# The first tile's output stored in pieces of 2, 11 and 12 tokens in place of 13 and 12, in a copy-and-scale kernel

## The chip, the cores and the metric

The kernel runs on one core of a Trainium2 chip. The metric is the device time of one execution in microseconds (us), the median of several runs. Engines that matter here: VectorE (DVE in the profile), ScalarE (ACT), and 16 DMA engines, which move all transfers. A transfer is issued from a queue: SP's (SyncE's, SPq in the profile, q1 in its DMA rows) or ACT's (ACTq, q10). "GB/s" counts bytes moved by all 16 DMA engines; MB are 10^6 bytes and KB in the rows of transfers 1,024 bytes.

## What is computed

```python
batch, seq, hidden, n_experts = 16, 1024, 512, 8
k = 2
# x: [16, 1024, 512] float32, expert_weights: [16, 1024, 2] float32
x_expanded = x[:, :, np.newaxis, :].repeat(k, axis=2)
weights = expert_weights[..., np.newaxis]
return (x_expanded * weights).astype(np.float32)
```

Each of 16,384 tokens is a row of 512 floats. It is written twice, scaled by each of its two weights. 33.55 MB are read and 67.11 MB written; expert_indices isn't used.

## The kernel before

**Tiles.** The tokens are spread over 128 partitions, 128 tokens to a partition. They are cut into five tiles of 25 tokens a partition (`groups`) and a rest of 3 (`LAST`). In what follows "a token" means one token on every partition: 2 KB of input and 4 KB of output on each. Transfers go by rows of one partition: a load of 25 tokens is 128 packets of 51,200 bytes, a store of 13 tokens 128 packets of 53,248.

**Memory.** Two input buffers (`x_pool`) take turns, so the load of tile i + 2 waits until tile i is multiplied. One output ring, `o_ring`, holds exactly 25 tokens of output; every tile writes the same places, so a piece of tile i + 1 can be multiplied only when the stores of tile i that read those places have landed. The rest has a buffer of its own for its input (`z_tile`), and its output goes to the start of the ring. The 128 weights pairs of a partition stand in `w_tile`.

**Loads.** `load` (L66 to L89) issues them on ACT's queue: tile 0 in pieces of 9 and 16 tokens (`FIRST`), tile 1 whole. Behind the first piece, `weights` issues the weights on SP's queue in three transfers: those of tile 0 (L97, 25 KB, 128 rows of 200 bytes), those of tiles 1 to 4 (L99, 100 KB, 512 rows of 200 bytes), those of the rest (L106, 3 KB, 128 rows of 24 bytes). Behind the multiplication of tile 0 ACT issues the load of tile 2 (L79) and that of the rest (L87, 768 KB, 128 rows of 6,144 bytes); a one-column copy (L76) keeps the latter behind tile 0.

**Multiplying and storing.** `emit` (L150 to L154) goes through the pieces of a tile, given as a list of cuts and a list of shares. `fill` has VectorE multiply the first `v` tokens of a piece, in instructions of up to 4 tokens (`CH`, L129), and ACT the others, one instruction for each token and weight (L119). Then SP issues the store of the piece (L154). Tiles 0 and 1 have pieces of 13 and 12 tokens, tiles 2 to 4 of 9, 8 and 8. Of the first 13 tokens VectorE takes 9 and ACT 4, of the next 12 VectorE 9 and ACT 3.

**Order.** Each engine runs its instructions in the order in which they stand; the framework adds the semaphore waits. For the transfers of SP and ACT it has eight completion semaphores, which the transfers take in turn. A transfer whose semaphore was last used by another one is issued only once that one has landed (where the engine doesn't know this already by an earlier wait).

The lines that matter most:

```python
    SHARES = [[9, 9], [9, 8], [9, 8, 8]]
...
    for i in range(2):
        load(i)
    for i, (done, n) in enumerate(tiles):
        cuts = [0, 13, n] if i < 2 else [0, 9, 17, n]
        emit(loaded[i], rows(of, done, n), done * k, cuts, SHARES[min(i, 2)])
        load(i + 2)
```

Of the kernel before, what the change touches and what calls it, by code (L numbers as in the profile page):

```python
# [1 line left out]

# [4 lines left out]


@with_exitstack
def kernel(  # L10
    ctx: ExitStack,
    tc: tile.TileContext,
    x: bass.AP,
    expert_indices: bass.AP,
    expert_weights: bass.AP,
    out: bass.AP,
):
    nc = tc.nc

    batch, seq, hidden = x.shape  # L20
    k = expert_weights.shape[-1]
    P = nc.NUM_PARTITIONS
    ntok = batch * seq
    assert ntok % P == 0
    A_TOTAL = ntok // P

    f32 = mybir.dt.float32
    row = k * hidden
    CH = 4


    groups = [25, 25, 25, 25, 25]
    TX = max(groups)
    LAST = 3
    FIRST = [9, 16]
    SHARES = [[9, 9], [9, 8], [9, 8, 8]]
    assert sum(groups) + LAST == A_TOTAL

    xf = x.rearrange("b s h -> (b s) h")
    of = out.rearrange("b s k h -> (b s) (k h)")  # L40
    wf = expert_weights.rearrange("b s k -> (b s) k")

    w_pool = ctx.enter_context(tc.tile_pool(name="w_pool", bufs=1))
    x_pool = ctx.enter_context(tc.tile_pool(name="x_pool", bufs=2))
    o_pool = ctx.enter_context(tc.tile_pool(name="o_pool", bufs=1))

    w_tile = w_pool.tile([P, A_TOTAL * k], f32)
    o_ring = o_pool.tile([P, TX * row], f32)

    def rows(of_all, done, T):  # L50
        return of_all[done * P : (done + T) * P, :].rearrange(
            "(p a) n -> p (a n)", a=T
        )


    if LAST:
        z_pool = ctx.enter_context(tc.tile_pool(name="z_pool", bufs=1))
        z_tile = z_pool.tile([P, LAST * hidden], f32)

    tiles = []  # L60
    done = 0
    for n in groups:
        tiles.append((done, n))
        done += n

    loaded = []  # L66

    def load(i):
        if i >= len(tiles):
            return  # L70
        done, n = tiles[i]
        x_tile = x_pool.tile([P, TX * hidden], f32)
        src = rows(xf, done, n)
        steps = FIRST if i == 0 else [n]
        if i == 2 and LAST:
            nc.scalar.copy(out=z_tile[:, :1], in_=o_ring[:, TX * row - 1 :])  # L76
        for e, step in enumerate(steps):
            at = sum(steps[:e])
            nc.scalar.dma_start(  # L79
                out=x_tile[:, at * hidden : (at + step) * hidden],  # L80
                in_=src[:, at * hidden : (at + step) * hidden],
            )
            if i == 0 and e == 0:
                for g in range(3):
                    weights(g)
        if i == 2 and LAST:
            nc.scalar.dma_start(out=z_tile, in_=rows(xf, A_TOTAL - LAST, LAST))  # L87
        loaded.append(x_tile)


    T0 = groups[0]
    G = len([n for n in groups[1:] if n == T0])
    head = (1 + G) * T0

    def weights(e):
        if e == 0:
            nc.sync.dma_start(out=w_tile[:, : T0 * k], in_=rows(wf, 0, T0))  # L97
        elif e == 1:
            nc.sync.dma_start(  # L99
                out=w_tile[:, T0 * k : head * k].rearrange("p (g n) -> p g n", g=G),  # L100
                in_=wf[T0 * P : head * P, :].rearrange(
                    "(g p a) n -> p g (a n)", g=G, p=P
                ),
            )
        else:
            nc.sync.dma_start(  # L106
                out=w_tile[:, head * k :], in_=rows(wf, head, A_TOTAL - head)
            )

    def product(engine, o_tile, t, x_in, c, m):  # L110

        o = t * row
        if engine is not None:
            for e in range(m * k):
                out_e = o_tile[:, o + e * hidden : o + (e + 1) * hidden]
                in_e = x_in[:, e // k * hidden : (e // k + 1) * hidden]
                w_e = w_tile[:, c + e : c + e + 1]
                if engine is nc.scalar or engine is nc.any and (c + e) % 3 == 2:
                    nc.scalar.mul(out=out_e, in_=in_e, mul=w_e)  # L119
                else:  # L120
                    nc.vector.tensor_scalar(
                        out=out_e,
                        in0=in_e,
                        scalar1=w_e,
                        scalar2=None,
                        op0=mybir.AluOpType.mult,
                    )
            return
        nc.vector.tensor_tensor(  # L129
            out=o_tile[:, o : o + m * row].rearrange(  # L130
                "p (t k h) -> p t k h", t=m, k=k
            ),
            in0=x_in[:, : m * hidden]
            .rearrange("p (t h) -> p t h", t=m)
            .unsqueeze(2)
            .to_broadcast([P, m, k, hidden]),
            in1=w_tile[:, c : c + m * k]
            .rearrange("p (t k) -> p t k", t=m)
            .unsqueeze(3)
            .to_broadcast([P, m, k, hidden]),  # L140
            op=mybir.AluOpType.mult,
        )

    def fill(o_tile, x_in, c, m, v):
        for t in range(0, v, CH):
            u = min(t + CH, v)
            product(None, o_tile, t, x_in[:, t * hidden : u * hidden], c + t * k, u - t)
        product(nc.scalar, o_tile, v, x_in[:, v * hidden :], c + v * k, m - v)

    def emit(src, dst, c, cuts, shares):  # L150
        for at, to, v in zip(cuts, cuts[1:], shares):
            o_tile = o_ring[:, at * row : to * row]
            fill(o_tile, src[:, at * hidden : to * hidden], c + at * k, to - at, v)
            nc.sync.dma_start(out=dst[:, at * row : to * row], in_=o_tile)  # L154

    for i in range(2):
        load(i)
    for i, (done, n) in enumerate(tiles):
        cuts = [0, 13, n] if i < 2 else [0, 9, 17, n]
        emit(loaded[i], rows(of, done, n), done * k, cuts, SHARES[min(i, 2)])  # L160
        load(i + 2)
    emit(
        z_tile,
        rows(of, A_TOTAL - LAST, LAST),
        (A_TOTAL - LAST) * k,
        [0, LAST],
        [LAST],
    )

# [1 line left out]
_INS = ['x', 'expert_indices', 'expert_weights']  # L171
_OUTS = [((16, 1024, 2, 512), 'float32')]


# [23 lines left out]
```

## Time and profile before

| | us |
|---|---|
| median of 3 runs | 239.63 |
| lowest and highest | 239.58 and 239.79 |
| the profiled execution | 239.66 |
| its span in the profile | 237.9 |
| VectorE busy | 123.8 |
| ACT busy | 20.2 |

The span runs from the first to the last instruction of the program. The page of the profile gives busy times by engine, rows of 40 equal slices of the span, the traffic of the DMA queues, the chain of work that ended last, groups of instructions by line with busy time, mean time and the idle time before them, and the transfers with the median time from issue to landing. A view of the traffic can be had for any window; in it a packet counts whole in the place where it starts, so a window of a few us that large packets straddle shows a rate that is too high or too low, and only windows of small packets or long windows can be read as rates. Lines such as L129 are those of the kernel listed above.

### The profile page before, as it was taken

How to read it: one execution, taken by the hardware profiler on the slowest of the kernel's cores; microseconds unless marked ns; L12 is line 12 of the kernel's file. 1: busy time of each engine (PE TensorE's matmuls, PEld its weight loads, DVE VectorE, ACT ScalarE, POOL GpSimd, SP SyncE). 2: the span in 40 equal slices, each digit the busy share in tenths (PEclk: the TensorE clock that was granted, in tenths of full speed). 3: DMA queues.
4: the chain of work that ended last, by engine and by line, in shares of the span. 5: the costliest groups of instructions: out<-in, count | busy, mean ns of one | idle time of the engine just before them, and what ended most of it. 6: DMA issues, size and time to landing. Idle time of an engine off the chain costs nothing.

```text
span 237.9 us, 167 instructions
## 1 busy us (share of the span) xinstructions
DVE 123.8 (52%) x33; ACT 20.2 (8%) x32; POOL 0.2 (0%) x4
## 2 busy tenths in 40 slices
DVE  0499800000059293089505999493096999865000
ACT  0008900000052160000000000000000000000000
POOL 0000000000000000000000000000000000000000
DMA  7999999999999999999999999899999999999996
GB/s 259 450 422 467 467 433 415 415 391 450 439 397 397 417 430 438 496 446 407 403 419 426 484 419 474 364 452 452 439 409 430 413 435 436 477 398 441 441 441 265
DMA packets 3840, 100.80 MB, mean 424 GB/s; under 512 B 1152, under 2 KB 1152, under 8 KB 1280
## 3 DMA queue, kind: packets, MB, share of 16 engines
q1 hardware_dynamic: 2832, 67.24, 65.7%
q10 hardware_dynamic: 1008, 33.55, 33.2%
HBM read 33.69 MB, written 67.11 MB: 424 GB/s over the span
## 4 chain that ended last, share of the span: by engine, by line
DMA 68%; DVE 18%; ACT 3%; issue 2%; ACTq 0%; DVEq 0%; SPq 0%
DMA out_dram<-o_ring 60%; DVE o_ring L129 18%; DMA x_tile<-in_x_dram 7%; ACT o_ring L119 2%; ACT L119 1%; ACTq L79 0%; DVEq L129 0%; SPq L154 0%; ACTq L119 0%
## 5 line engine op out<-in xcount | busy, mean ns | idle before, releaser
L129 DVE TENSOR_TENSOR o_ring<-x_tile,w_tile 128x4096 f32<-128x4096 f32 (+1 forms) x32 | 120.4, 3820 | 91.6 <-DMA out_dram<-o_ring 69.8
L119 ACT ACTIVATE o_ring<-x_tile,w_tile 128x512 f32<-128x512 f32 x30 | 18.7, 708 | 48.1 <-DMA out_dram<-o_ring 48.0
L129 DVE TENSOR_TENSOR o_ring<-z_tile,w_tile 128x3072 f32<-128x3072 f32 x1 | 3.4, 3360 | 2.1 <-DMA out_dram<-o_ring 2.1
L119 ACT ACT_TABLE_LOAD x1 | 1.3, 1283 | 19.0 <-DMA x_tile<-in_x_dram 19.0
L76 ACT COPY z_tile<-o_ring 128x1 f32<-128x1 f32 x1 | 0.2, 191 | 0.0
L182 POOL MEMSET const-bfloat16-1.0<- 128x1 bf16 x1 | 0.1, 102 | 0.0
L182 POOL MEMSET const-uint8-127<- 128x1 uint8 x1 | 0.1, 102 | 0.0
L182 POOL MEMSET const-float32-0.0<- 128x1 f32 x1 | 0.1, 99 | 0.2 <-issue 0.2
L182 POOL MEMSET const-float32-1.0<- 128x1 f32 x1 | 0.1, 99 | 0.0
## 6 DMA issues: line engine op xcount, KB each, us to landing
x_tile<-in_x_dram ACTq DMA_DIRECT2D x4, 6400.0 KB, 30.5
out_dram<-o_ring SPq DMA_DIRECT2D x6, 4096.0 KB, 21.5
out_dram<-o_ring SPq DMA_DIRECT2D x3, 4608.0 KB, 26.8
out_dram<-o_ring SPq DMA_DIRECT2D x2, 6656.0 KB, 33.1
out_dram<-o_ring SPq DMA_DIRECT2D x2, 6144.0 KB, 44.8
x_tile<-in_x_dram ACTq DMA_DIRECT2D x1, 4096.0 KB, 17.8
x_tile<-in_x_dram ACTq DMA_DIRECT2D x1, 2304.0 KB, 8.3
out_dram<-o_ring SPq DMA_DIRECT2D x1, 1536.0 KB, 19.5
```

Of the source, the lines that this page charges most:

```text
L76: nc.scalar.copy(out=z_tile[:, :1], in_=o_ring[:, TX * row - 1 :])
L119: nc.scalar.mul(out=out_e, in_=in_e, mul=w_e)
L129: nc.vector.tensor_tensor(out=o_tile[:, o : o + m * row].rearrange("p (t k h) -> p t k h", t=m, k=k), in0=x_in[:, : m * hidden] .rearrange ...
L182: nc = _bacc.Bacc("TRN2", target_bir_lowering=False, num_devices=1)
```

## The change

Tile 0 is stored in three pieces, of 2, 11 and 12 tokens. VectorE multiplies both tokens of the first piece and 7 of the 11 of the second, ACT the other 4 of these; the 12 tokens stay as they were. The cuts move into a list beside the shares. In all, VectorE multiplies 18 tokens of tile 0 and ACT 7, as before.

```diff
     FIRST = [9, 16]
-    SHARES = [[9, 9], [9, 8], [9, 8, 8]]
+    CUTS = [[0, 2, 13, 25], [0, 13, 25], [0, 9, 17, 25]]
+    SHARES = [[2, 7, 9], [9, 8], [9, 8, 8]]
     assert sum(groups) + LAST == A_TOTAL
...
     for i, (done, n) in enumerate(tiles):
-        cuts = [0, 13, n] if i < 2 else [0, 9, 17, n]
-        emit(loaded[i], rows(of, done, n), done * k, cuts, SHARES[min(i, 2)])
+        form = min(i, 2)
+        emit(loaded[i], rows(of, done, n), done * k, CUTS[form], SHARES[form])
         load(i + 2)
```

All lines behind the new one move down by one (L129 becomes L130, L154 becomes L155). In the compiled program:

- VectorE's first three instructions of tile 0 are of 2,048, 4,096 and 3,072 elements a partition in place of 4,096, 4,096 and 1,024; the others are the same. ACT's instructions are the same.
- SP issues 15 stores in place of 14: 8,192 and 45,056 bytes a partition in place of 53,248, the others as before. The first waits for VectorE alone, the second for VectorE and ACT, as the one of 13 tokens did.
- VectorE's first instruction of tile 1 waits for both stores.
- The transfers take other semaphores from there on. The load of the rest (L88), which had that of the first weights (25 KB), has that of the second (100 KB), and its issue waits for them.

The semaphores, numbered 0 to 7, with the transfers that take each in order (t1a is the first store of tile 1, and so on; s2, s11, s12 and s13 are the stores of tile 0 by their tokens; x3 is the load of tile 3):

| | before | after |
|---|---|---|
| 0 | x0 (9), s12, t2c | x0 (9), x2, x4, last store |
| 1 | weights 25 KB, rest's load, t3a | weights 25 KB, s12, t2c |
| 2 | weights 100 KB, t1a, t3b | weights 100 KB, rest's load, t3a |
| 3 | weights 3 KB, x3, t3c | weights 3 KB, t1a, t3b |
| 4 | x0 (16), t1b, t4a | x0 (16), x3, t3c |
| 5 | x1, t2a, t4b | x1, t1b, t4a |
| 6 | s13, t2b, t4c | s2, t2a, t4b |
| 7 | x2, x4, last store | s11, t2b, t4c |

## The prediction

> **What bounds the kernel now.** I read the head of the page first, then the timeline of the first 70 us, the transfers, and last the DMA traffic of chosen windows. The page's span, VectorE's share and the two DMA rows (40 slices of 5.95 us: busy tenths, then GB/s):
>
> ```profile
> span 237.9 us, 167 instructions
> DVE 123.8 (52%) x33; ACT 20.2 (8%) x32; POOL 0.2 (0%) x4
> ...
> DMA  7999999999999999999999999899999999999996
> GB/s 259 450 422 467 467 433 415 415 391 450 439 397 397 417 430 438 496 446 407 403 419 426 484 419 474 364 452 452 439 409 430 413 435 436 477 398 441 441 441 265
> ```
>
> The 16 DMA engines are busy in every slice; VectorE is busy for half the span. So no compute and no issue is the bound: the kernel ends when the bytes are through, and a change of the time must come from bytes, from the rate of some stretch, or from the two ends. The execution took 239.66 us for its span of 237.9; the median of the runs is 239.63, 0.03 lower.
>
> The timeline of the first 70 us (start, duration, engine; ACTq and SPq are the queues that issue transfers):
>
> ```profile
> 0.72 1.43 ACTq L79 DMA_DIRECT2D x_tile<-in_x_dram  x3
> 0.72 0.37 SPq L97 DMA_DIRECT2D w_tile<-in_expert_weights_dram  x1
> 1.15 0.43 SPq L99 DMA_DIRECT2D w_tile<-in_expert_weights_dram  x1
> 1.62 0.50 SPq L106 DMA_DIRECT2D w_tile<-in_expert_weights_dram  x1
> 9.05 19.77 DVE L129 TENSOR_TENSOR o_ring<-x_tile,w_tile 128x4096 f32<-128x4096 f32 x6 [9.05 <-DMA x_tile<-in_x_dram]
> ...
> 20.27 8.68 ACT L119 ACTIVATE o_ring<-x_tile,w_tile 128x512 f32<-128x512 f32 x14
> 25.30 4.02 SPq L154 DMA_DIRECT2D out_dram<-o_ring  x2
> ...
> 29.05 0.34 ACTq L79 DMA_DIRECT2D x_tile<-in_x_dram  x1
> 29.43 0.46 ACTq L87 DMA_DIRECT2D z_tile<-in_x_dram  x1
> 67.82 2.56 ACT L119 ACTIVATE o_ring<-x_tile,w_tile 128x512 f32<-128x512 f32 x4 [38.65 <-DMA out_dram<-o_ring]
> 67.83 4.42 DVE L129 TENSOR_TENSOR o_ring<-x_tile,w_tile 128x4096 f32<-128x4096 f32 x1 [39.01 <-DMA out_dram<-o_ring]
> ```
>
> The first store is issued at 25.30, but that isn't when it moves. The transfers (line, queue, KB, us from issue to landing), and the traffic from 20 to 48 us (q1 is SP's queue, q10 ACT's: packets, MB, time share):
>
> ```profile
> w_tile<-in_expert_weights_dram SPq DMA_DIRECT2D x1, 100.0 KB, 48.6
> w_tile<-in_expert_weights_dram SPq DMA_DIRECT2D x1, 25.0 KB, 5.5
> w_tile<-in_expert_weights_dram SPq DMA_DIRECT2D x1, 3.0 KB, 50.5
> ```
>
> ```profile
> DMA packets 502, 11.93 MB, mean 426 GB/s; under 512 B 270, under 2 KB 270, under 8 KB 270
> ## 3 DMA queue, kind: packets, MB, share of 16 engines
> q10 hardware_dynamic: 248, 11.88, 98.2%
> q1 hardware_dynamic: 254, 0.05, 0.9%
> ```
>
> From 20 to 48 us SP's queue moves 254 packets of 0.05 MB, weights of some 200 B, one for each of the 248 big packets of ACT's queue. The two take turns packet by packet. So the 100 KB of weights (512 rows) land at 1.15 + 48.6 = 49.75 us and the last 3 KB at 1.62 + 50.5 = 52.1, and the stores issued at 25.30 and after wait behind them until about 51. That decides what an earlier store can do.
>
> Then a stretch stands out. The traffic from 48.9 to 50.7 us, and from 100 to 217 us:
>
> ```profile
> DMA packets 144, 0.44 MB, mean 243 GB/s; under 512 B 73, under 2 KB 73, under 8 KB 144
> ## 3 DMA queue, kind: packets, MB, share of 16 engines
> q10 hardware_dynamic: 72, 0.44, 92.9%
> q1 hardware_dynamic: 72, 0.00, 2.2%
> ```
>
> ```profile
> DMA packets 1478, 50.50 MB, mean 432 GB/s; under 512 B 175, under 2 KB 175, under 8 KB 175
> ```
>
> Here rows of z_tile's load (6,144 B, q10) take turns with the last weights (24 B) at 243 GB/s, where the long stretch of loads and stores goes at 432. The engines count as busy, yet a z row takes 0.929 x 16 x 1.8 / 72 = 0.37 us. Against 432 GB/s this stretch loses 1.8 x (1 - 243/432) = **0.79 us**, the one dip I find behind the start.
>
> **The change, part by part.** *The early store* (2 tokens, 1 MB). Its product is one VectorE instruction from 9.05 us. Shapes by line:
>
> ```profile
> L129 DVE TENSOR_TENSOR o_ring<-x_tile,w_tile 128x4096 f32<-128x4096 f32 x26 | 113.8, 4420 | 91.6 <-DMA out_dram<-o_ring 69.8 <-issue 12.8 <-DMA x_tile<-in_x_dram 9.1
> L129 DVE TENSOR_TENSOR o_ring<-x_tile,w_tile 128x1024 f32<-128x1024 f32 x6 | 7.3, 1218 | 0.0
> L129 DVE TENSOR_TENSOR o_ring<-z_tile,w_tile 128x3072 f32<-128x3072 f32 x1 | 3.4, 3360 | 2.1 <-DMA out_dram<-o_ring 2.1
> ```
>
> 2,048 elements are not in the trace: halfway between 1,218 and 3,360 ns is 2,289. The store is then issued near 9.05 + 2.3 = 11.4 us, 14 us earlier, and moves nothing: it stands behind the weights until about 49. Worth 0. If it did get through early, it would only trade places with loads on engines that are already full. VectorE's first 13 tokens cost 2,289 + 4,420 + 3,360 = 10,069 ns in place of 2 x 4,420 + 1,218 = 10,058: 0.01 us, covered by ACT's eight activations, on which the store at 25.30 waits. Without that cover it would be 0.01 us. The 11 tokens are issued at 25.30 as the 13 were, and the second tile's first instructions now wait for both stores, whose bytes together are the old ones: 0.
>
> *One more transfer.* 128 more packets, 8 to an engine, and one more issue (0.35 us on SP's queue, idle between 2.1 and 25.30, nothing behind it). What a packet costs beside its bytes, from rows of 12 KB alone at the end (233.08 to 236.1 us) against large rows (131 to 232 us):
>
> ```profile
> DMA packets 106, 1.29 MB, mean 427 GB/s; under 512 B 1, under 2 KB 1, under 8 KB 1
> ...
> DMA packets 1368, 43.81 MB, mean 434 GB/s; under 512 B 144, under 2 KB 144, under 8 KB 144
> ```
>
> 1.6% of 12,288 B at 27 GB/s an engine (455 ns) is 7 ns; 8 x 7 = **+0.06 us**, on the path because the DMA engines are. Bounds: 0, and 0.13 at twice that for the smaller rows.
>
> The Trainium skill's page "DMA: Bandwidth & Descriptors", section "Anatomy of one DMA", speaks against this piece: it gives each transfer a fixed 2.0 us, mostly the receipt of its last write. By that the sum below would be 239.0 + 2.0 = 241.0. The stretch from 100 to 217 us, with its 432 GB/s across the ends of some ten transfers, shows that here the next transfer's bytes cover it.
>
> *The moved semaphores.* The added transfer shifts the turn in which transfers take the eight completion semaphores. As compiled, z's load takes the one of the 100 KB of weights where it took that of the 25 KB. Its issue at 29.43, which found its semaphore free, must now wait for those weights: until about 49.7 us, or a little less without z beside them. Behind it on ACT stand the second tile's activations, which wait for the first stores until 67.82: 18 us of cover. If that were gone, ACT's stall of 20 us would reach the load of the fourth tile. z's rows are read only here:
>
> ```profile
> 214.16 3.36 DVE L129 TENSOR_TENSOR o_ring<-z_tile,w_tile 128x3072 f32<-128x3072 f32 x1 [2.13 <-DMA out_dram<-o_ring]
> ```
>
> so z itself may be late by 150 us. The other new pairs of transfers on one semaphore are as far apart as the old ones.
>
> What the delay does to the DMA engines is the term that matters. When the third tile's load ends (by 48.9 its large packets have given way to z's rows, as that window shows), ACT's queue is empty. The last weights have the engines to themselves, then come the 8 KB rows of the early store, and z's rows join at about 50.5, among store rows. The dip's pairing of z rows with 24 B rows is gone: **-0.79 us** if all is regained, 0 if none. Against it stands a gap where the last weights run alone with nothing large to fill the engines. The nearest rows for weights that run with little beside them are from 1.7 to 2.46 us, at the start, and, for 24 B rows just ahead of store rows, from 50.7 to 51.4 us:
>
> ```profile
> DMA packets 71, 0.14 MB, mean 187 GB/s; under 512 B 64, under 2 KB 64, under 8 KB 64
> ...
> DMA packets 119, 0.83 MB, mean 1187 GB/s; under 512 B 76, under 2 KB 76, under 8 KB 107
> ```
>
> The first loses 0.76 x (1 - 187/432) = 0.43 us, from a standing start. The second has 76 tiny packets and shows no loss (packets count whole where they start, hence 1,187). So the gap is 0 to 0.43; the second row is nearer, since requests are already under way, and I take +0.1.
>
> Sum: 239.66 - 0.79 + 0.06 + 0.1 = **239.0 us**, the end being reached earlier because every later store and load runs on full engines. Bounds: 239.66 - 0.79 + 0 + 0 = 238.9, and 239.66 - 0.79 + 0.13 + 0.43 = 239.4; the dip's blurred edges may add 0.2 below.
>
> **The rivals.** *Nothing gained.* The dip is not a matter of z and 24 B rows but of passing from loads to the first store: reads for 53 KB store rows begin while z's rows are still coming. For it: the dip ends where the store's rows begin. Against it: in the late part, loads join stores with no dip. Then the loss returns at the new hand-over, and the time is 239.66 + 0.07 = 239.7. The same time comes out if z's issue is not delayed at all.
>
> *Slower: the 24 B rows are the slow thing.* If each holds its engine, whatever else is queued, 0.79 us x 16 engines / 72 rows = 0.18 us a row, then 8 of them in series on each engine, with no z row to fill in, cost 1.4 us each time they are alone: 239.66 - 0.79 + 1.4 + 0.07 = 240.3. It decides if the rate between 48.5 and 50 falls below 243 GB/s. Against it: the 270 packets under 512 B from 20 to 48 us went by at 426 GB/s in all. The Trainium skill's same page, section "Specifications", says that below 512 B a transfer does a read-modify-write, which would suit this rival; the 200 B rows are below 512 B too and show no such loss.
>
> *Slower: each transfer pays a fixed end.* The end of the 2-token store holds the engines before the 11 tokens start. The time from last byte to landing is not hidden then; the last store bounds its size: its rows still start in the window that ends at 236.1, and the span ends at 237.9, so 1.8 us at most. Time 239.66 - 0.79 + 0.07 + 1.8 = 240.7 at most. Against it stands the 432 GB/s of the long stretch.
>
> **How the numbers follow.** Forecast 0.68; nothing gained 0.23; slow 24 B rows 0.06; fixed end 0.03. About 0.2% (0.48 us) is what a measurement of this kernel can tell from no change, so faster begins below 239.15. Of the forecast's own range, 238.7 to 239.4, about three quarters of the chance lies below that, because only a gap near its upper bound lifts it over: 0.50 faster, 0.18 same. With the first rival, same is 0.41; slower is 0.09. The range for 8 in 10 reaches from 238.6 past the first rival to 239.85, which leaves out the two slower cases and the tails.
>
> **What would show it.** Right: the first store issued near 11.4 us but SP's queue still at 0.05 MB from 20 to 48; z's load issued near 49.5 in place of 29.43; traffic between 48.9 and 50.7 above 400 GB/s; the second tile's VectorE work at about 67.2 in place of 67.83, and everything behind it earlier by the same 0.6. Wrong: z's load still issued at 29.4; or a stretch near 49 us as slow as the old one; or a start of the second tile that is early while the end is not, which would mean a new dip later on.

## The result, and the profile after

| | before | changed |
|---|---|---|
| median of 22 runs each, us | 239.68 | 240.27 |
| lowest and highest, us | 239.46 and 240.09 | 239.56 and 240.91 |
| the profiled execution, us | 239.66 | 240.44 |
| its span, us | 237.9 | 238.7 |

The ratio of changed to before is 1.0018, 95% interval 1.0010 to 1.0026 (the two medians alone would give 1.0025): slower, by a little less than the 0.2% that the prediction took as what can be told from no change. In three later comparisons, each on a chip of its own (11 runs of the changed kernel each), the medians were 0.36, 0.06 and 0.07 us over those of the kernel before, with ratios of 1.0009, 1.0005 and 1.0004, whose intervals all reach 1.0000 or below. The 0.6 us of gain that was forecast appeared nowhere. Of the runs further below, three of the six of e6 were in a slower state, and its ratio leaves them out.

The head of the changed kernel's page: the span, VectorE, and the DMA rows of 40 slices.

```profile
span 238.7 us, 169 instructions
...
DVE 123.8 (52%) x33; ACT 20.2 (8%) x32; POOL 0.2 (0%) x4
...
DMA  7999999999999999999999999999999999999995
GB/s 264 464 450 457 439 414 414 414 404 414 427 426 412 488 455 425 431 403 404 412 508 400 408 434 458 431 406 434 433 432 436 439 434 449 402 462 434 428 397 251
```

As before, the DMA engines are busy throughout. The timeline of its first 70 us:

```profile
8.84 19.76 DVE L130 TENSOR_TENSOR o_ring<-x_tile,w_tile 128x2048 f32<-128x2048 f32 x6 [8.84 <-DMA x_tile<-in_x_dram]
11.16 17.93 SPq L155 DMA_DIRECT2D out_dram<-o_ring  x3
...
28.83 0.34 ACTq L80 DMA_DIRECT2D x_tile<-in_x_dram  x1
50.31 0.33 ACTq L88 DMA_DIRECT2D z_tile<-in_x_dram  x1
67.80 2.56 ACT L120 ACTIVATE o_ring<-x_tile,w_tile 128x512 f32<-128x512 f32 x4 [38.85 <-DMA out_dram<-o_ring]
67.84 4.43 DVE L130 TENSOR_TENSOR o_ring<-x_tile,w_tile 128x4096 f32<-128x4096 f32 x1 [39.24 <-DMA z_tile<-in_x_dram]
```

The early store is issued at 11.16, and the rest's load at 50.31 in place of 29.43, as the moved semaphore demands. (The last line's z_tile is the profile's guess from a semaphore that z shares with the weights. The rest landed 19.0 us after its issue, at 69.3, so VectorE didn't wait for it; ACT's line beside it names the stores.) But the second tile starts at 67.84, where it started at 67.83. By then both kernels have moved nearly the same transfers, so up to there nothing was gained and nothing lost. The traffic from 20 to 48 us shows the early store still waiting behind the weights, as in the kernel before:

```profile
q10 hardware_dynamic: 245, 11.72, 99.9%
q1 hardware_dynamic: 244, 0.05, 0.9%
```

**Where the dip went.** From 49.8 to 51.4 us, where z's rows had crawled, the rows of the early store run at 420 GB/s:

```profile
DMA packets 82, 0.67 MB, mean 420 GB/s; under 512 B 0, under 2 KB 0, under 8 KB 0
```

In the window of the prediction, 48.9 to 50.7 us, the traffic is this, where it was 243 GB/s and more than 400 was to be the sign of the gain:

```profile
DMA packets 284, 0.66 MB, mean 365 GB/s; under 512 B 205, under 2 KB 205, under 8 KB 205
```

Large rows that started before 48.9 us still run into this window and aren't counted in it. So the old dip is gone, and a new one stands right ahead of it. In the window from 46.2 to 47.05 us the last rows of the third tile's load start, one on each engine (16 packets on q10). The view gives the time of the packets that start in it as a share of 16 engines' window. First the kernel before, then the changed one:

```profile
q10 hardware_dynamic: 16, 0.82, 224.3%
```

```profile
q10 hardware_dynamic: 16, 0.82, 320.3%
```

2.243 x 0.85 = 1.91 us for one row before, 3.203 x 0.85 = 2.72 us after. The last row of each engine takes 0.82 us longer: the size of the loss that was to be saved (0.79). The loss has only moved from z's rows to the row ahead.

**Where the time grew.** VectorE's later pieces, released by landed stores; the timeline before, then after:

```profile
127.66 22.90 DVE L129 TENSOR_TENSOR o_ring<-x_tile,w_tile 128x4096 f32<-128x4096 f32 x6 [11.69 <-DMA out_dram<-o_ring]
...
173.01 8.76 DVE L129 TENSOR_TENSOR o_ring<-x_tile,w_tile 128x4096 f32<-128x4096 f32 x2 [10.40 <-DMA out_dram<-o_ring]
```

```profile
127.97 22.90 DVE L130 TENSOR_TENSOR o_ring<-x_tile,w_tile 128x4096 f32<-128x4096 f32 x6 [12.13 <-DMA out_dram<-o_ring]
...
173.75 8.76 DVE L130 TENSOR_TENSOR o_ring<-x_tile,w_tile 128x4096 f32<-128x4096 f32 x2 [10.54 <-DMA out_dram<-o_ring]
...
214.90 3.36 DVE L130 TENSOR_TENSOR o_ring<-z_tile,w_tile 128x3072 f32<-128x3072 f32 x1 [2.12 <-DMA out_dram<-o_ring]
```

The lag behind the kernel before is 0.01 us at 67.8, 0.31 at 128, 0.74 at 173 and 0.74 at 214. It comes up in the stretch where the loads of the fourth and fifth tile run beside stores, far from the changed lines.

A landing is told by 16 semaphore increments, one from each DMA engine, and VectorE waits for the last of them. The trace has the time of each. For the last store of the program, in us:

```
profiled run         its time   mean landing   last landing   last - mean
before                 239.66         236.78         237.06          0.29
changed                240.44         236.85         237.81          0.96
changed again (r)      240.45         236.73         237.81          1.08
changed again (f1)     240.19         236.85         237.56          0.71
changed again (g4)     240.11         236.89         237.48          0.59
```

Each time is the last landing plus 2.60 to 2.64 us. The mean landing is the same within 0.16 us. These are single executions: those of r, f1 and g4 took 0.22 to 0.32 us more than the medians of their runs. What grew in them is the distance of the slowest engine from the others: each of the 16 has 8 of a transfer's 128 rows to move by itself, and the kernel ends with the last of them. The end of the trace's traffic shows it without the semaphores: rows that start from 236.3 to 237.5 us, before and after.

```profile
DMA packets 13, 0.00 MB, mean 0 GB/s; under 512 B 13, under 2 KB 13, under 8 KB 13
```

```profile
DMA packets 16, 0.04 MB, mean 31 GB/s; under 512 B 13, under 2 KB 13, under 8 KB 13
```

Before, only completion packets are left by then. After, three rows of 12 KB are still to come, on engines that lag.

### The profile page after: what moved, and what is told of

It is laid out like the page before. It is cut to its first block, busy times and chain, and to the rows that moved or that the text cites. A ratio compares the mean times of both kernels' runs of the same rounds, so it can differ in the third digit from the quotient of the medians.

```text
span 238.7 us, 169 instructions
## 1 busy us (share of the span) xinstructions
DVE 123.8 (52%) x33; ACT 20.2 (8%) x32; POOL 0.2 (0%) x4
## 4 chain that ended last, share of the span: by engine, by line
DMA 66%; DVE 22%; another core or an unknown queue 2%; issue 1%; SPq 0%; DVEq 0%; ACTq 0%
DMA out_dram<-o_ring 38%; DVE o_ring L130 22%; DMA w_tile<-in_expert_weights_dram 21%; DMA z_tile<-in_x_dram 7%; SPq L98 0%; DVEq L130 0%; SPq L155 0%; ACTq L88 0%
## 5 line engine op out<-in xcount | busy, mean ns | idle before, releaser
L130 DVE TENSOR_TENSOR o_ring<-x_tile,w_tile 128x4096 f32<-128x4096 f32 (+3 forms) x32 | 120.4, 3820 | 92.4 <-DMA out_dram<-o_ring 44.3
L130 DVE TENSOR_TENSOR o_ring<-z_tile,w_tile 128x3072 f32<-128x3072 f32 x1 | 3.4, 3357 | 2.1 <-DMA out_dram<-o_ring 2.1
## 6 DMA issues: line engine op xcount, KB each, us to landing
x_tile<-in_x_dram ACTq DMA_DIRECT2D x4, 6400.0 KB, 30.8
```

What stands on the lines that cost most here:

```text
L130: nc.vector.tensor_tensor(out=o_tile[:, o : o + m * row].rearrange("p (t k h) -> p t k h", t=m, k=k), in0=x_in[:, : m * hidden] .rearrange ...
```

## The experiments

Each time is the median of 11 runs (12 for e7 and g1, 4 for e5; for e6 the lowest and highest of 6) beside runs of the kernel before on the same chip. The ratio is that of the measurement and not of the two medians.

| run | tile 0's pieces | rest's load | us | before, us | ratio, 95% interval |
|---|---|---|---|---|---|
| e1_split_rest_early | 2, 11, 12 | early | 239.94 | 239.72 | 1.0008 (0.9999 to 1.0018) |
| e2_whole_rest_late | 13, 12 | late | 239.85 | 239.72 | 1.0004 (0.9995 to 1.0013) |
| e3_whole_order | 13, 12 | early | 239.85 | 239.72 | 1.0008 (1.0000 to 1.0017) |
| e4_split_6_7_12 | 6, 7, 12 | late | 239.94 | 239.72 | 1.0010 (1.0001 to 1.0019) |
| r_changed_again | 2, 11, 12 | late | 240.14 | 239.78 | 1.0009 (1.0000 to 1.0018) |
| e5_one_weight_row_whole | 13, 12 | early | 245.12 | 239.78 | 1.0228 (1.0210 to 1.0246) |
| e6_one_weight_row_split | 2, 11, 12 | early | 240.82 to 245.43 | 239.78 | 1.0103 (1.0052 to 1.0153) |
| e7_pool_weights_split | 2, 11, 12 | early | 240.11 | 239.78 | 1.0015 (1.0005 to 1.0025) |
| f1_changed | 2, 11, 12 | late | 239.87 | 239.81 | 1.0005 (0.9996 to 1.0014) |
| f2_split_rest_early | 2, 11, 12 | early | 240.06 | 239.81 | 1.0013 (1.0004 to 1.0022) |
| f3_whole_rest_late | 13, 12 | late | 239.80 | 239.81 | 1.0002 (0.9992 to 1.0011) |
| f4_whole_order | 13, 12 | early | 239.94 | 239.81 | 1.0003 (0.9994 to 1.0012) |
| g1_pool_weights_whole | 13, 12 | early | 240.42 | 239.82 | 1.0030 (1.0014 to 1.0047) |
| g2_pool_weights_split | 2, 11, 12 | early | 240.01 | 239.82 | 1.0013 (0.9996 to 1.0029) |
| g3_pieces_13_10_2 | 13, 10, 2 | early | 240.06 | 239.82 | 1.0008 (0.9999 to 1.0017) |
| g4_changed | 2, 11, 12 | late | 239.89 | 239.82 | 1.0004 (0.9995 to 1.0012) |

**One part of the change at a time: e1 to e4.** The first theory, A, was that the late load of the rest takes its small rows out of the passage from loads to stores, so that the stall falls unevenly on large rows. The second, B, was that the 2-token piece itself does it.

e1, against the changed kernel (the rest's load shares its semaphore with weights that land early):

```diff
-                for g in range(3):
+                for g in (0, 2, 1):
                     weights(g)
```

> The changed kernel, with the order of the two later weight transfers exchanged, so that the rest's load shares its semaphore with the 3 KB of weights (landed by some 12 us) and is issued near 29 us again. Theory A (the delay of the rest's load takes its small rows out of the passage from loads to stores, the stall there falls unevenly on one large row of each DMA engine, and the slowest engine ends later): about 239.7, the last store's landings as close as in the kernel before (0.5 us from first to last engine). Theory B (the 2-token piece itself does it: one more transfer, 8 KB rows): about 240.3 as the changed kernel.

e2, against the kernel before (one more transfer moves the semaphores as the split does):

```diff
-            nc.sync.dma_start(
-                out=w_tile[:, head * k :], in_=rows(wf, head, A_TOTAL - head)
-            )
+            for lo in (0, P // 2):
+                nc.sync.dma_start(
+                    out=w_tile[lo : lo + P // 2, head * k :],
+                    in_=rows(wf, head, A_TOTAL - head)[lo : lo + P // 2, :],
+                )
```

> The kernel before, tile 0 still in pieces of 13 and 12, with the 3 KB of weights loaded as two transfers of 64 partitions each: the same rows, one more transfer, which moves the rest's load to the semaphore of the 100 KB of weights, so that it is issued near 50 us. Theory A: about 240.2, as the changed kernel, with the third tile's last rows at about 2.7 us in place of 1.9 and landings of the last store about 1 us apart. Theory B: about 239.7.

e3 is e1's edit in the kernel before:

> The kernel before with the order of the two later weight transfers exchanged, as a control for the first: the rest's load stays near 29 us and its rows meet 200 B rows of weights in place of 24 B rows. Theory A and B: 239.7, no change. If 24 B rows are what is slow at the passage, about 239.1 (the 0.6 to 0.8 us of the old dip gone).

e4, against the changed kernel:

```diff
-    CUTS = [[0, 2, 13, 25], [0, 13, 25], [0, 9, 17, 25]]
-    SHARES = [[2, 7, 9], [9, 8], [9, 8, 8]]
+    CUTS = [[0, 6, 13, 25], [0, 13, 25], [0, 9, 17, 25]]
+    SHARES = [[6, 3, 9], [9, 8], [9, 8, 8]]
```

> The changed kernel with pieces of 6, 7 and 12 tokens: the same semaphores and the same late rest's load, first rows of 24 KB in place of 8 KB. Theory A: as the changed kernel, about 240.2. Theory B in its form that the 8 KB rows do it: nearer 239.7.

None reached 240.2, so the time alone decided nothing between A and B. The traces did for the dip. The same window as above, 46.2 to 47.05 us, in e2 and then in e1:

```profile
q10 hardware_dynamic: 16, 0.82, 318.5%
```

```profile
q10 hardware_dynamic: 16, 0.82, 226.9%
```

e2 stores 13 tokens first, and its last load rows take 3.185 x 0.85 = 2.71 us, as in the changed kernel. So it is the late rest that moves the dip, not the 2-token piece. Where the rest is early (e1), the rows take 1.93 us and the dip sits in the rest's rows. For e4, with its 24 KB rows:

```profile
q10 hardware_dynamic: 16, 0.82, 329.1%
```

2.80 us. To add the dip up I took, from the packets of each trace, the time by which rows took longer than is usual for their size (the 20th percentile of that size), over all 16 engines, from 44 to 53 us:

```
before 12.9   changed 13.3   e1 10.8   e2 13.1   e3 12.5   e4 14.5   r 12.2   f1 14.5   f2 9.0   f3 15.6   f4 12.3   g3 9.9   g4 9.7
```

9 to 16 engine-us, or 0.6 to 1.0 us an engine, whatever stands there: rest's rows beside 24 B weights, beside 200 B weights (e3, f4), or large load rows beside 200 B weights; store rows of 8, 24 or 53 KB behind. e3 rules out the 24 B rows as the cause, e2 and f3 the meeting of rest and weights. What all of them share is that the first store's rows are taken up there. But they also share that small weight rows come before these, and that the loads end there; e7 and g1 below have neither.

**The changed kernel again, and an early store that gets through: r, e5, e6, e7.**

> The changed kernel once more, unaltered, on the chip of the next runs. Theory S (the engines lose the same 13 engine-us at the passage as before, and the time moves only with how far the 16 engines part; the 2-token piece has no price of its own): 239.9, as with pieces of 6, 7 and 12. Theory P (the 2-token piece costs): 240.2 to 240.3 again.

It was 240.14, 0.36 over the kernel before, between the two theories.

e5 and e6 change the spread of the tokens in the kernel before and in the changed one:

```diff
     def rows(of_all, done, T):
-        return of_all[done * P : (done + T) * P, :].rearrange(
-            "(p a) n -> p (a n)", a=T
-        )
+        n = of_all.shape[1]
+        return of_all.rearrange("(p a) n -> p (a n)", a=A_TOTAL)[
+            :, done * n : (done + T) * n
+        ]
...
-                for g in range(3):
-                    weights(g)
+                nc.sync.dma_start(out=w_tile, in_=rows(wf, 0, A_TOTAL))
```

> The kernel before (13 and 12) with another spread of the tokens: each partition has 128 tokens that follow each other, so that all its weights are one row of 1 KB and one transfer of 128 rows replaces three of 768. The store issued at 25 us then finds SP's queue empty and moves at once, among loads. If only the small weight rows go: 640 rows x 15 ns / 16 engines = 0.6 us less, 239.1. If the loss at the passage belongs to z's rows or to the end of the loads: another 0.8 us less, 238.3. If the larger step between the rows of a transfer (256 KB of x, 512 KB of output) slows the traffic: over 245.

> The same with the pieces of 2, 11 and 12: the first store moves near 12 us. Against the one with 13 and 12: the same within 0.2 us, since the DMA engines are full either way (my view of the early store in the prediction); or 0.3 us or more less, if stores that start early spare the passage its loss.

e5's four runs took 244.7 to 246.1 us. Of e6's six, two took about 241 us and four 244 to 245. In e5 the traffic from 26 to 62 us, where loads and stores run side by side, is at 393 GB/s:

```profile
DMA packets 302, 14.14 MB, mean 393 GB/s; under 512 B 31, under 2 KB 31, under 8 KB 31
```

Large rows stall there by up to 1.5 us, in several bursts. Since the spread itself moves the time by so much, the two can't be read for what an early store is worth. e7 can: it keeps the old spread, and the two later weight transfers of the changed kernel go by GpSimd's queue.

```diff
-            nc.sync.dma_start(
+            nc.gpsimd.dma_start(
                 out=w_tile[:, T0 * k : head * k].rearrange("p (g n) -> p g n", g=G),
...
-            nc.sync.dma_start(
+            nc.gpsimd.dma_start(
                 out=w_tile[:, head * k :], in_=rows(wf, head, A_TOTAL - head)
             )
```

> The changed kernel with the two later weight transfers issued from GpSimd's queue in place of SP's: SP's queue is free and the 2-token store moves near 12 us with the old spread of the tokens. If an early store gains nothing and the passage costs its 0.8 us wherever it lies: 239.7 to 240.3. If the early store spares it: 239.0 to 239.4.

Its traffic from 12 to 28 us, and the rows that start from 30.1 to 30.8:

```profile
DMA packets 272, 6.82 MB, mean 426 GB/s; under 512 B 16, under 2 KB 16, under 8 KB 16
## 3 DMA queue, kind: packets, MB, share of 16 engines
q10 hardware_dynamic: 160, 5.90, 86.5%
q1 hardware_dynamic: 112, 0.92, 13.5%
```

```profile
q10 hardware_dynamic: 16, 0.82, 327.4%
```

Now SP's queue moves 0.92 MB by 28 us: the early store is really early. The dip comes early too, in parts: 16 load rows take 3.274 x 0.7 = 2.29 us each in place of 1.9 at 30 us, and with those near 15 us the sum is 9.6 engine-us from 12 to 44 us, none from 44 to 53. Only a third of it (3.0) stands in the load rows beside the 2-token store's first rows, which start at 15.8 us. The rest (6.4) stands in the last load row of each engine ahead of the second store's 45 KB rows, which start at 32.5. So the loss goes with the beginning of the stores, the second one's too where loads still run, and isn't spared; the time was 240.11.

**Two by two on one chip: f1 to f4.** Theory L says that the late rest costs, P that the 2-token piece costs, D that neither does more than shift the queues.

> The changed kernel (2-token piece, rest's load late), the corner of a table of two by two, all on one chip with the kernel before (13 and 12, rest's load early). So far it was 0.59 and 0.36 us over the kernel before, on two chips. Both theories: 240.0 to 240.3, the mean landing of the last store over the 16 engines as before within 0.15 us (236.6 to 236.9) and the last engine 0.9 us or more behind the mean.

> Split, rest's load early (weights in the other order). Theory L (the late load of the rest makes it slower): 239.8, as the kernel before. Theory P (the 2-token piece makes it slower): 240.1 as the changed kernel. Theory D (neither; any shift of the queues parts the engines a little more than the kernel before does): 239.9, between the two, as the whole one with late rest.

> Whole, rest's load late (3 KB of weights in two transfers). Theory L: 240.1 as the changed kernel. Theory P: 239.7 to 239.8, as the kernel before. Theory D: 239.9.

> Whole, rest's load early, weights in the other order: the control for the split one with early rest. L and P: 239.75, as the kernel before. D: 239.9.

Measured: 239.87, 240.06, 239.80 and 239.94 beside 239.81. L falls: the late rest with whole pieces is as fast as the kernel before within the interval, twice (e2, f3). The split is 0.06 and 0.25 over it; all intervals overlap. f1 itself missed what both theories had for it: it was to take 240.0 at least, with the last engine 0.9 us or more behind the mean, and that was 0.71. So this table decides nothing between P and D.

**The same away from the passage: g1 to g4.** g1 is e7's edit in the kernel before, g2 is e7 again, g4 the changed kernel. g3, against the changed kernel:

```diff
-    CUTS = [[0, 2, 13, 25], [0, 13, 25], [0, 9, 17, 25]]
-    SHARES = [[2, 7, 9], [9, 8], [9, 8, 8]]
+    CUTS = [[0, 13, 23, 25], [0, 13, 25], [0, 9, 17, 25]]
+    SHARES = [[9, 8, 1], [9, 8], [9, 8, 8]]
```

> The kernel before (13 and 12) with the two later weight transfers on GpSimd's queue. Against g2 (2, 11 and 12 with the same): if the 2-token piece itself parts the engines, 0.2 to 0.3 us less than g2, some 239.8; if not, the same as g2, some 240.1.

> The changed kernel with the two later weight transfers on GpSimd's queue, once more, for g1 on the same chip: 240.1, as before (0.33 us over the kernel before).

> Tile 0 in pieces of 13, 10 and 2 tokens, in that order, the rest's load early as in the kernel before. If it is the 2-token piece at the passage that costs: 239.8, the price of 128 more packets alone (0.06 us). If one more transfer anywhere parts the engines: 240.0 or more, as g4.

> The changed kernel on the chip of g3: 0.1 to 0.5 us over the kernel before, mean landing of the last store unchanged within 0.15 us, the last engine 0.7 us or more behind it.

g3 was 240.06 and g4 239.89, beside 239.82. No run here shows that the 2 tokens as the first rows are what costs: with the small piece behind the passage the time was no lower. But both intervals reach below 1, so it isn't shown either that these two cost anything. g4 was to be 0.1 us or more over the kernel before, with the last engine 0.7 us or more behind; it was 0.07 and 0.59. g1, without any split, was slower than g2 (240.42 against 240.01), the reverse of what P asked for, though their intervals overlap.

g1 shows the loss at its plainest. One store of 53 KB rows begins at 30.1 us while the second tile's load still runs, with no weights ahead of it. The 20 load rows that start from 26.2 to 29.4 us take 0.888 x 16 x 3.2 / 20 = 2.27 us each in place of 1.89 (88.8% is their share of 16 engines' window), and no packet of SP's queue starts there. So neither the end of the loads nor the small rows make the loss.

**What the engines' distance says.** Last minus mean landing of the last store, in the profiled runs that keep the old spread of tokens and SP's weights:

```
whole pieces:  before 0.29   e2 0.31   e3 0.53   f3 0.39   f4 0.41
split pieces:  changed 0.96   r 1.08   f1 0.71   g4 0.59   e1 0.51   f2 0.70   e4 0.43   g3 0.74
```

The means are 0.39 and 0.72 us; the mean landing itself is 236.64 to 236.89 in all 13. The difference, 0.33 us, is most of what parts these executions: their times are 239.74 and 240.15 us in the mean. Over all runs it is less: the medians of the eight with split pieces lie 0.06 to 0.59 us over that of the kernel before (0.25 in the mean), those of the four changed ones with whole pieces -0.01 to 0.13 (0.10). Nor does whole always mean close: g1's profiled run, with GpSimd's weights, has 2.42.

The slowest engine's packets can be followed back, since each starts where the one before it ends, to 4 ns. Where several engines are as close as that, the path isn't the only one, so sums at the passage are rough. In the changed kernel its rows lost 1.0 to 1.2 us at the passage, by the path taken, and about 0.75 in load rows from 103 to 157 us; in the kernel before 0.7 to 1.0 in z's rows and 0.38 in one load row at 101 us. In e1 a single load row at 146 us lost 0.74, in e2 one at the same place 0.61, and both made their engine the last. Its last row ended 0.18 and 0.08 us behind the next engine's, so that most of each stall cost nothing: what it costs goes by how far the others are.

## Why the prediction was wrong

- **The early store is worth nothing by itself.** Right: issued at 11.16 (11.4 was forecast), 0.05 MB on SP's queue from 20 to 48 us. e7, where it does get through, is no faster either.
- **128 more packets, +0.06 us.** The mean landing moved by +0.07 in the first profile and by -0.05 to +0.11 in the others of the changed kernel. That isn't against it, but the term is too small to be shown.
- **The late load of the rest.** Issued at 50.31, a little behind the 49.5 to 49.7 forecast, and covered as said: ACT's next work came at 67.80.
- **The step that failed is "-0.79 us if all is regained"** for the dip between 48.9 and 50.7 us. The pairing of z rows with 24 B rows did go, as the prediction said; the loss was put down to that pairing and isn't bound to it. The runs show 0.6 to 1.0 us an engine where the first store's rows are taken up, with or without z rows, with 24 B or 200 B rows, with store rows of 8, 24 or 53 KB. Where the stores are early it is early too, without any weights beside it (g1), and then in two parts if the first store is small (e7, 0.6 in all). With z's rows gone it fell on the last rows of the third tile's load, 2.72 us in place of 1.91.
- **The gap at the hand-over, +0.1,** was sought behind the last weights. From 49.8 us on no gap stood there (420 GB/s). The loss stood one row ahead, in rows that the kernel before moved in 1.91 us, and since these rows ran on behind 48.9, the window from there reached 365 GB/s and not the 400 that was to show the gain.
- **The rival "nothing gained"** told what happened, a loss that returns at the new hand-over, and the place that spoke for it (the dip ends where the store's rows begin). Its reason, that store rows are read ahead, is not shown. What I held against it, that later loads join stores without a dip, doesn't bear on the first store. Its 239.7 is missed in the first comparison (240.27), since neither it nor any other case had the engines' distance; 239.87 and 239.89 (f1, g4), beside 239.81 and 239.82, are near it.
- **What is missing from all cases:** the time is set by the slowest of 16 engines, and stalls of single rows, 0.3 to 1.2 us, don't cancel out for it. In the first two profiles that was 0.67 (0.96 less 0.29) of the 0.78 us between them, with the mean landing 0.07 later.
- **The two slower rivals** fell. The 24 B rows ran off at once when alone: 420 GB/s stands right behind them, and the loss is there without them (e3, g1). A fixed end of each transfer would have moved the mean landing by up to 1.8 us. The Trainium skill's page "DMA: Bandwidth & Descriptors", section "Anatomy of one DMA", has 2.0 us for each transfer on GpSimd's path. The transfers here go by SP's and ACT's queues, and on these, full as they are, one more transfer moved the mean landing by 0.11 us at most.

The failed term explains why nothing was gained. Why the changed kernel was slower still is open: why, and whether at all, split pieces set the engines further apart. The late rest alone doesn't do it (e2, f3), and neither first rows of 24 KB nor a small piece put last brought the time lower (e4, g3). With one profile for each run, the difference of 0.39 and 0.72 us may in part be chance, and the changed kernel's own excess went from 0.06 to 0.59 us between comparisons. Open too is what in the DMA engines makes the loss at the passage; that they read store rows ahead while load rows are still coming would fit, and was not tried by itself. No version here was clearly faster than the kernel before.

## What to carry to other kernels

A dip beside small rows need not be theirs: before booking it as a gain, ask whether it marks a passage that the kernel must go through anyway, and what would stand in it if those rows went. A store issued early moved here only when its queue's earlier transfers had, and on full DMA engines even one that moved early gained nothing (e7). Where all DMA engines are busy to the end, look at the slowest engine beside the mean: differences of a few tenths of a microsecond between single executions were made there.

## What the runs showed of the hardware

- 512 weight rows of 200 B, 0.1 MB in all, landed 48.6 us after their issue and held SP's queue until then: the two queues took turns packet by packet (254 packets against 248 from 20 to 48 us), with rows of 51 KB on the other.
- With rows that follow each other at a step of 256 KB (x) and 512 KB (output) from partition to partition, the kernel took 2.3% longer (e5) or 1.0% (e6). The step wasn't tried by itself, but the early store alone, in the old spread, cost 0.3% (g1).
- Load rows just ahead of the first store's rows lost time, 9 to 16 us in the sum over 16 engines in 13 profiles: one such row took 2.72 us in place of 1.91 in the changed kernel, and 2.27 in place of 1.89 in g1.
- The excess of one and the same kernel over the kernel before was 0.06 to 0.59 us in four comparisons. The ratios of two of them, 1.0005 and 1.0004, lie outside the first one's interval of 1.0010 to 1.0026, though their own intervals, up to 1.0014 and 1.0012, reach into it.
